# Two pads of a kernel's SBUF layout, 128 bytes shorter each

## The chip, the cores and the metric

The kernel runs on one core of a Trainium2 chip. The metric is device microseconds of one execution; lower is better. The time before is the median of three runs. The profile is of one further execution, whose own time stands beside it.

## The reference

The kernel computes a small decoder trunk on a residual stream x of 512 positions by 1024 features, in float32: one layer with a gated short convolution, one with forgetting attention, each followed by a feed-forward network (FFN) with a convolution.

```python
def short_conv_mixer(xn, w_in, conv_w, w_out):
    b, c, h = jnp.split(xn @ w_in, 3, axis=-1)
    return (b * causal_dwconv(c * h, conv_w)) @ w_out

def conv_ffn(xn, w_up, conv_w, w_down):
    a, g = jnp.split(xn @ w_up, 2, axis=-1)
    return (jax.nn.silu(causal_dwconv(a, conv_w)) * g) @ w_down
...
# layer 0: x += short_conv_mixer(rmsnorm(x)); x += conv_ffn(rmsnorm(x))
# before layer 1: k, v and the forget gate's cumulative decay c, all from h = rmsnorm(x)
# layer 1: x += (forgetting_attention(q, k, v, c) * sigmoid(gate)) @ w_out; x += conv_ffn(rmsnorm(x))
```

There are 16 heads of 64; the FFN is 2816 wide. Attention is a causal softmax of `q k / 8 + c_i - c_j`.

## The kernel before, in words

**Arithmetic.** TensorE multiplies float32 operands in a rounded form (F32R). To keep the precision, every operand is split into a rounded part `hi` and the rest `lo = x - hi`, and a product is three matmuls: hi x hi, hi x lo and lo x hi. ScalarE makes `hi` (a copy) and VectorE makes `lo` (a subtraction). For weights this is done in `parts` (L148 and L149), from a tile `raw` that a DMA filled.

**The matmuls.** Activations lie transposed, features on partitions and 512 positions along the row. `mac` (L164 to L166) adds one 128x128 block of weights times 128 features into a PSUM bank, in two halves of 256 columns, three matmuls each:

```python
nc.tensor.matmul(ps[:, f], lhsT=lh[0], rhs=rh[0][:, f], ...)   # L164
nc.tensor.matmul(ps[:, f], lhsT=lh[0], rhs=rh[1][:, f], ...)   # L165
nc.tensor.matmul(ps[:, f], lhsT=lh[1], rhs=rh[0][:, f], ...)   # L166
```

`lhsT` is the weights' tile that is loaded into the array, `rhs` the data that move through it. Every matmul loads its weights anew. The output projections of the mixer and of both FFNs use seven products in place of eight (`Seven`, the matmuls in `go`, L440 to L442, again three of 256 columns each, with weight splits at L423 and L424).

**Stages.** (1) The first three blocks of the mixer run as x arrives: weights are split into tiles of the pools g and gl, the moving data are the normed inputs n. (2) The rest of the mixer, its output projection, and the FFN of layer 0: weights in the pool w; the moving data are n for the input and up projections and g and gl for the output and down projections (each FFN has three down projections, after 7, 15 and 22 of the 22 column blocks of the up projection). (3) Attention: V is projected first, and there the roles are exchanged. The normed inputs n are the weights (slices of 128 columns) and the split weights, in pools whi and wlo, move, into four PSUM banks in turn. Then K, q and the gate are projected as in stage 2 with weights in whi and wlo and n or g as moving data, between the scores, the softmax and the products with V. (4) The FFN of layer 1, as in stage 2, with weights in w.

**Layout.** Pools take SBUF one behind the other, in the order in which they are opened. Those opened first stay: const, misc (m, ld), small, norm (tiles n, 2048 bytes per partition), raw (4096). Behind raw comes a set of pools for each stage, named with its number of tiles in `stage(...)`. A name that starts with pad is not a pool of tiles but so many bytes per partition that nothing uses. Tiles of g, gl, pt, s, whi and wlo have 2048 bytes per partition and those of w and sum 4096, all multiples of 256, as are the steps of a slice inside a tile (128 columns are 512 bytes). So where a tile starts modulo 256, counted from n, is set by the pads ahead of it alone.

**Order.** Outside of attention the order of the instructions of ScalarE, VectorE and GpSimd is held as written (`in_order`). `Line` loads weights and splits them some units ahead of their use (up to 12 tiles of w). TensorE takes the matmuls in the order in which they are written.

Of the kernel before, what the change touches and what calls it, by code (L numbers as in the profile page):

```python
# [57 lines left out]
def trunk(ctx: ExitStack, tc: tile.TileContext, x_t, a_in, a_out, up0, down0, wk, wv, wf, wqg, b_out,  # L58
# [14 lines left out]
    def stage(*sizes):  # L73

        pools = ExitStack()
        pool.clear()
        for name, bufs in sizes:
            if name.startswith("pad"):
                pools.enter_context(tc.tile_pool(name=name, bufs=1)).tile([P, bufs // 4], F32, tag=name,
                                                                          name=f"{name}_{len(pool)}_{len(sizes)}")  # L80
                continue
            pool[name] = pools.enter_context(tc.tile_pool(name=name, bufs=bufs))
        return pools
# [10 lines left out]
    def GL(dtype=F32):  # L94
        return new(pool["gl" if "gl" in pool else "g"], "gl" if "gl" in pool else "g", [P, T], dtype)
# [27 lines left out]
    pr = const.tile([P, NPAR], F32, tag="pr", name="pr")  # L123
    cs = const.tile([P, C_ET], F32, tag="cs", name="cs")

    pools = stage(("g", 16), ("sum", 4), ("gl", 16), ("pad", 192), ("w", 12))
    x = [GL() for _ in range(KT)]
    ones = const.tile([P, P], F32R, tag="ones", name="ones")
    nc.vector.memset(ones.bitcast(F32), 1.0)
# [158 lines left out]
    @contextmanager  # L288
    def in_order(*engines):

        traced = nc.cur_bb.bb.instructions
        n = len(traced)
        yield
        for eng in engines:
            own = [i for i in list(traced)[n:] if i.engine == eng.engine]
            for a, b in zip(own[:-1], own[1:]):
                tc.add_manual_dep(b, a.name, mybir.DependencyInfo(mybir.DependencyClass.NoSync,
                                                                  mybir.DependencyReason.DATA), reason="in order")
# [319 lines left out]
    def ffn_line(line, up, down):  # L618

        seq, k0 = [], 0  # L620
        for j in range(JT):
            seq.append(("up", j, [line.add(One(up[j, c])) for c in range(2)]))
            if j in (6, 14, JT - 1):
                n = (j + 1) // 2 - k0
                seq.append(("down", j, Project(line, [z[:, 4 * k0 * P:4 * (k0 + n) * P] for z in down], n)))
                k0 += n
        return seq

    def ffn(seq, col, norm, nxt, last=False):
        r = None  # L630
        us, late = [], None
        for kind, j, w in seq:
            if kind == "down":
                if j < JT - 1:
                    w.run(us, None)
                    us = []
                else:
                    late()
                    w.run(us, nxt, last=last, hold=True)
                continue  # L640
            if late:
                late()
                late = None
            if j == 0:
                pa, pg = gemm2(w, norm.xs, between=norm.fold)
                r, _ = norm.finish()
            else:
                pa = gemm(w[0], norm.xs)
            if j == JT - 1:
                part = seq[-1][2]  # L650
                part.prefetch()
            a = M()
            nc.vector.tensor_tensor(out=a, in0=pa, in1=r, op=ALU.mult)  # L653
            y = conv(a, col + 3 * j)
            act_silu(out=y, in_=y, func=AF.Silu)
            if j > 0:
                pg = gemm(w[1], norm.xs, j == JT - 1)
            g = M()
            nc.vector.tensor_tensor(out=g, in0=pg, in1=r, op=ALU.mult)  # L659
            if j % 2 == 0:  # L660
                f = S()

            def late(g=g, y=y, j=j, f=f):
                end = j == JT - 1
                (nc.vector if end else nc.gpsimd).tensor_tensor(out=half(f, j), in0=g, in1=y, op=ALU.mult)  # L665
                if j % 2:
                    us.append(operands(f, part.sevens[0].line.step if end else None))
# [481 lines left out]
        ffn(seq, PC_F[0], n2, n3)  # L1149
    pools.close()  # L1150
    n4 = Norm("ffn1")
    with stage(("pt", 6), ("s", 10), ("pad", 192), ("whi", 4), ("wlo", 4), ("pad2", 320), ("g", 40)):
        attention(n3, n4)
    with stage(("pad", 192), ("w", 12), ("pad2", 320), ("sum", 4), ("g", 16), ("gl", 16)):
        with in_order(*pinned):
            ffn(ffn_line(Line(12, 4), up1, down1), PC_F[1], n4, None, last=True)

# [76 lines left out]
```

## Time and profile before

| what | value |
|---|---|
| median of three runs | 1301.84 us (1297.83 to 1303.04) |
| profiled execution | 1303.14 us |
| its span, first to last instruction | 1301.4 us |
| mean granted TensorE clock | 0.978 of 2.4 GHz |
| TensorE busy | 1240.6 us, 95% of the span, 10113 matmuls |
| VectorE busy | 921.7 us, 71% |
| ScalarE busy | 593.7 us, 46% |
| GpSimd busy | 431.5 us, 33% |
| DMA | 151.40 MB, mean 116 GB/s |

The busy time of TensorE is a union of overlapping instructions: a matmul is recorded for some 280 ns, while the next one starts some 118 ns behind it. So busy time tells where TensorE has work; its pace is the distance of one start from the next. In a group's row `out<-in,in` names the tiles: the written one, then the moving one, then the weights.

### The profile page before, as it was taken

What the parts mean: (1) busy time and instruction counts of PE and PEld (TensorE: products, weight loads), DVE (VectorE), ACT (ScalarE), POOL (GpSimd) and SP (SyncE); (2) the same over time, 40 slices, a digit from 0 to 9 for tenths busy, and PEclk for the clock granted to TensorE, in tenths of its full rate; (3) what the DMA queues carried; (4) which work ended last, traced back from release to release, by engine and by line L of the source; (5) the groups of instructions that cost most, each with busy time, mean ns of one, the idle gap of its engine ahead of it and who ended that gap; (6) DMA issues with size and microseconds to landing.
All of it is one profiled execution on the core that took longest, in us unless ns stands there. A gap on an engine that the chain in (4) does not pass through costs nothing.

```text
span 1301.4 us, 24422 instructions
## 1 busy us (share of the span) xinstructions
PE 1240.6 (95%) x10113; PEld 1205.5 (93%) x10113; DVE 921.7 (71%) x1274; ACT 593.7 (46%) x972; POOL 431.5 (33%) x319
## 2 busy tenths in 40 slices
PE   8999989999999999869999989999999999999997
PEld 8999978999999999869998878889999999999987
DVE  6755696778667866785636778876567867776677
ACT  6322354344434443443456677774434433343422
POOL 0113371234135414470022354542023612361244
PEclk9999998999999999998999899999999999999989
DMA  7331154227323632253233222225421752164213
GB/s 273 106 108 66 50 181 159 70 62 268 115 72 97 223 119 66 81 162 117 86 106 119 80 68 65 66 82 174 151 86 38 229 168 82 49 216 160 63 50 121
DMA packets 54352, 151.40 MB, mean 116 GB/s; under 512 B 6049, under 2 KB 6561, under 8 KB 54241
## 3 DMA queue, kind: packets, MB, share of 16 engines
q1 hardware_dynamic: 53456, 148.47, 35.7%
q8 instruction: 79, 1.29, 0.4%
q10 hardware_dynamic: 720, 1.18, 0.2%
q14 instruction: 33, 0.26, 0.1%
q0 software_dynamic: 64, 0.20, 0.0%
HBM read 133.01 MB, written 16.81 MB: 115 GB/s over the span
## 4 chain that ended last, share of the span: by engine, by line
PE 71%; DVE 16%; ACT 6%; issue 3%; POOL 2%; DMA 1%; SPq 0%; DVEq 0%; ACTq 0%; POOLq 0%
PE st L166 11%; PE st L164 11%; PE st L165 11%; PE mm L164 8%; PE mm L166 8%; PE mm L165 8%; DVE w L424 6%; PE st L442 3%; PE st L440 2%; PE st L441 2%; DVE gl L555 2%; PE mm L442 1%; PE mm L440 1%; PE mm L441 1%; ACT s L305 1%
## 5 line engine op out<-in xcount | busy, mean ns | idle before, releaser
L164 PE MATMUL st<-n,w 128*128 128x256 f32 x1216 | 342.1, 281 | 3.7 <-ACT n L272 2.5
L166 PE MATMUL st<-n,w 128*128 128x256 f32 x1216 | 341.6, 281 | 0.8 <-DVE w L149 0.8
L165 PE MATMUL st<-n,w 128*128 128x256 f32 x1216 | 341.4, 281 | 0.2 <-DVE n L273 0.2
L164 PEld LDWEIGHTS st<-n,w 128*128 128x128 f32 x1216 | 229.9, 189 | 4.2 <-ACT n L272 2.7
L166 PEld LDWEIGHTS st<-n,w 128*128 128x128 f32 x1216 | 230.5, 190 | 1.0 <-DVE w L149 1.0
L165 PEld LDWEIGHTS st<-n,w 128*128 128x128 f32 x1216 | 229.8, 189 | 0.6 <-DVE n L273 0.5
L665 POOL TENSOR_TENSOR sum<-m,m 128x512 f32<-128x512 f32 x42 | 64.6, 1538 | 341.7 <-DVE m L659 273.2
L149 DVE TENSOR_TENSOR w<-raw,w 128x1024 fp32r<-128x1024 f32 x109 | 133.1, 1240 | 56.9 <-ACT w L148 56.8
L164 PE MATMUL mm<-n,w 128*128 128x256 f32 x528 | 147.6, 280 | 0.0
L166 PE MATMUL mm<-n,w 128*128 128x256 f32 x528 | 147.5, 279 | 0.0
L165 PE MATMUL mm<-n,w 128*128 128x256 f32 x528 | 147.3, 279 | 0.0
L440 PE MATMUL st<-g,w 128*128 128x256 f32 x460 | 131.0, 285 | 13.8 <-ACT m L453 11.9
L442 PE MATMUL st<-g,w 128*128 128x256 f32 x460 | 131.0, 285 | 3.6 <-DVE w L424 3.6
L148 ACT CAST w<-raw 128x1024 fp32r<-128x1024 f32 x109 | 111.1, 1042 | 50.8 <-DMA raw<-up 18.5
L470 ACT ACTIVATE m<-m,pr 128x512 f32<-128x512 f32 x52 | 37.7, 724 | 175.1 <-DVE m L653 137.2
L441 PE MATMUL st<-gl,w 128*128 128x256 f32 x393 | 111.1, 283 | 0.0
L440 PEld LDWEIGHTS st<-g,w 128*128 128x128 f32 x460 | 87.9, 191 | 15.4 <-ACT m L453 13.3
L166 PEld LDWEIGHTS mm<-n,w 128*128 128x128 f32 x528 | 99.2, 188 | 0.0
L165 PEld LDWEIGHTS mm<-n,w 128*128 128x128 f32 x528 | 99.0, 187 | 0.0
L164 PEld LDWEIGHTS mm<-n,w 128*128 128x128 f32 x528 | 99.0, 187 | 0.0
L376 ACT CAST g<-sum 128x512 fp32r<-128x512 f32 x78 | 48.4, 621 | 107.5 <-POOL sum L665 64.3
L424 DVE TENSOR_TENSOR w<-sum,w 128x1024 fp32r<-128x1024 f32 (+1 forms) x56 | 85.5, 1540 | 13.0 <-ACT w L423 13.0
(221 smaller groups left out, 3322.9 us busy)
## 6 DMA issues: line engine op xcount, KB each, us to landing
raw<-up SPq DMA_DIRECT2D x88, 512.0 KB, 4.3
ld<-xsp SPq DMA_DIRECT2D x64, 256.0 KB, 4.0
raw<-down SPq DMA_DIRECT2D x32, 512.0 KB, 3.6
xsp<-gl SPq DMA_DIRECT2D x48, 256.0 KB, 3.4
raw<-a_in SPq DMA_DIRECT2D x21, 512.0 KB, 4.4
raw<-wqg SPq DMA_DIRECT2D x16, 512.0 KB, 3.6
raw<-down SPq DMA_DIRECT2D x16, 384.0 KB, 3.2
raw<-a_out SPq DMA_DIRECT2D x8, 512.0 KB, 4.0
```

The costliest lines, as they stand in the source:

```text
L148: nc.scalar.copy(out=hi[:, :w], in_=raw[:, c0:c1])
L149: nc.vector.tensor_tensor(out=lo[:, :w], in0=raw[:, c0:c1], in1=hi[:, :w].bitcast(F32), op=ALU.subtract)
L164: nc.tensor.matmul(ps[:, f], lhsT=lh[0], rhs=rh[0][:, f], start=go, stop=False, skip_group_check=True)
L165: nc.tensor.matmul(ps[:, f], lhsT=lh[0], rhs=rh[1][:, f], start=False, stop=False, skip_group_check=True)
L166: nc.tensor.matmul(ps[:, f], lhsT=lh[1], rhs=rh[0][:, f], start=False, stop=end, skip_group_check=True)
L376: nc.scalar.copy(out=blocks(hi), in_=src)
L424: nc.vector.tensor_tensor(out=lo[:, 0:n], in0=raw[:, 0:n], in1=hi[:, 0:n].bitcast(F32), op=ALU.subtract)
L440: nc.tensor.matmul(ps, lhsT=wh, rhs=xh, start=m in "17" and p == 0, stop=False, skip_group_check=True)
L441: nc.tensor.matmul(ps, lhsT=wh, rhs=xl, start=False, stop=False, skip_group_check=True)
L442: nc.tensor.matmul(ps, lhsT=wl, rhs=xh, start=False, stop=p == self.n - 1, skip_group_check=True)
L470: nc.scalar.activation(out=y, in_=src, func=AF.Copy, scale=pr[:, col + 2:col + 3])
L665: (nc.vector if end else nc.gpsimd).tensor_tensor(out=half(f, j), in0=g, in1=y, op=ALU.mult)
```

## The change

All three sets of pools change, and in them only the pads: 64 bytes in place of 192, and 192 in place of 320 for the second pad. Tiles of w, whi and wlo lie 128 bytes lower by it, and in the last two stages those behind the second pad 256 bytes lower. The code of the computation is the same.

```diff
-    pools = stage(("g", 16), ("sum", 4), ("gl", 16), ("pad", 192), ("w", 12))
+    pools = stage(("g", 16), ("sum", 4), ("gl", 16), ("pad", 64), ("w", 12))
...
-    with stage(("pt", 6), ("s", 10), ("pad", 192), ("whi", 4), ("wlo", 4), ("pad2", 320), ("g", 40)):
+    with stage(("pt", 6), ("s", 10), ("pad", 64), ("whi", 4), ("wlo", 4), ("pad2", 192), ("g", 40)):
         attention(n3, n4)
-    with stage(("pad", 192), ("w", 12), ("pad2", 320), ("sum", 4), ("g", 16), ("gl", 16)):
+    with stage(("pad", 64), ("w", 12), ("pad2", 192), ("sum", 4), ("g", 16), ("gl", 16)):
```

## Rows read from the trace of the kernel before

**Rows 1.** The chain that ended last, shares of the span by engine, tile, line.

```profile
by line: PE st L166 10.8%; PE st L164 10.8%; PE st L165 10.7%; PE mm L164 8.0%; PE mm L166 7.9%; PE mm L165 7.9%; DVE w L424 5.9%; issue 3.4%; PE st L442 2.5%; PE st L440 2.5%; PE st L441 2.4%; DVE gl L555 1.8%; PE mm L442 1.4%; PE mm L440 
```

**Rows 2.** Span of the core and its mean granted TensorE clock.

```profile
core 0: 1301.4 us, clock 0.978
```

**Rows 3.** By stretch: length; PE, PEld, DVE, ACT, POOL busy (instructions); clock; DMA.

```profile
33.00:140.00 107.00, 107.00 (x909) 106.92 (x908) 63.23 (x80) 33.29 (x43) 22.44 (x12) 1.00 0.27 88
304.00:390.00 86.00, 85.31 (x724) 85.31 (x725) 61.88 (x76) 33.60 (x46) 19.91 (x14) 1.00 0.44 144
410.00:518.00 108.00, 107.19 (x897) 107.19 (x898) 77.03 (x89) 46.40 (x63) 38.98 (x25) 0.98 0.44 138
634.00:700.00 66.00, 66.00 (x530) 62.44 (x529) 35.35 (x53) 38.36 (x70) 12.61 (x9) 1.00 0.37 113
...
880.00:985.00 105.00, 103.07 (x855) 102.46 (x854) 66.73 (x82) 44.92 (x65) 21.64 (x15) 0.98 0.41 131
1026.00:1110.00 84.00, 83.62 (x710) 83.62 (x711) 60.18 (x76) 32.66 (x45) 19.89 (x14) 1.00 0.46 146
1132.00:1238.00 106.00, 105.51 (x884) 105.51 (x885) 74.43 (x89) 45.64 (x62) 38.44 (x24) 0.98 0.44 140
...
0.00:22.00 22.00, 17.91 (x107) 16.09 (x108) 14.91 (x28) 14.61 (x23) 0.93 (x5) 0.92 0.86 312
...
577.00:593.00 16.00, 6.91 (x38) 6.75 (x37) 12.23 (x17) 3.61 (x6) 5.33 (x5) 0.68 0.62 194
```

**Rows 4.** TensorE's waits: who waited for whom, us in total, times, longest.

```profile
PE st L164 <- ACT w L148: 1.2, 1, 1.2
...
PE st L166 <- DVE w L149: 0.8, 1, 0.8
```

**Rows 5.** Timeline of TensorE in the first mixer: start, duration; first and last.

```profile
22.66 0.28 PE L165 MATMUL st<-n,g 128*128 128x256 f32 x1
...
27.09 0.28 PE L166 MATMUL st<-n,gl 128*128 128x256 f32 x1
```

**Rows 6.** The same in the rest of the mixer, first and last.

```profile
59.74 0.28 PE L165 MATMUL st<-n,w 128*128 128x256 f32 x1
...
65.98 0.28 PE L164 MATMUL st<-n,w 128*128 128x256 f32 x1
```

**Rows 7.** The same in the projection of V, first and last.

```profile
611.81 0.28 PE L164 MATMUL st<-whi,n 128*128 128x256 f32 x1
...
617.93 0.28 PE L164 MATMUL st<-whi,n 128*128 128x256 f32 x1
```

**Rows 8.** Line L165 by tiles: duration ns min/median/max, first and last start.

```profile
L165 PE MATMUL st<-n,w x1216: 276/279/583, 27.7 to 1246.7; 128*128 128x256 f32 x174
...
L165 PE MATMUL mm<-n,whi x288: 276/279/415, 637.7 to 857.6; 128*128 128x256 f32 x144
...
L165 PE MATMUL st<-wlo,n x64: 276/276/415, 589.3 to 631.0; 128*128 128x256 f32 x64
...
L165 PE MATMUL st<-n,g x32: 280/283/415, 8.9 to 27.3; 128*128 128x256 f32 x32
```

**Rows 9.** Timeline of TensorE right behind the first mixer, first and last.

```profile
27.58 0.28 PE L164 MATMUL st<-n,w 128*128 128x256 f32 x1
...
32.45 0.28 PE L165 MATMUL st<-n,w 128*128 128x256 f32 x1
```

**Rows 10.** The chain from 0 to 27.6 us, shares of that stretch.

```profile
by line: DMA g<-a_in 21.3%; PE st L164 16.0%; PE st L166 14.5%; PE st L165 14.1%; PE mm L166 7.6%; PE mm L164 7.2%; PE mm L165 6.8%; ACT g L266 4.5%; SPq L1113 1.5%; SPq L1110 1.5%; SPq L1115 1.4%; issue 1.0%
```

**Rows 11.** The chain from 587 to 634 us (V), shares of that stretch.

```profile
by line: PE mm L165 17.5%; PE mm L166 16.6%; PE st L165 16.3%; PE mm L164 16.3%; PE st L166 16.2%; PE st L164 15.4%; DMA m<-cst 8.1%; PE st L736 0.7%; PE at L353 0.5%; PE at L352 0.5%
```

**Rows 12.** Splits on VectorE by line: duration ns min/median/max, first and last start.

```profile
L149 DVE TENSOR_TENSOR wlo<-raw,whi x64: 673/693/1789, 626.6 to 906.9; 128x512 fp32r<-128x512 f32 x64
...
L377 DVE TENSOR_TENSOR gl<-sum,g x78: 676/684/691, 53.7 to 1255.6; 128x512 fp32r<-128x512 f32 x78
```

**Rows 13.** The chain from 143 to 200 us, shares of that stretch.

```profile
by line: DVE w L424 23.3%; issue 13.6%; DVE gl L555 12.1%; DVE n L273 7.4%; DMA ld<-xsp 6.0%; DVE m L461 5.2%; DVE gl L564 4.9%; ACT n L272 3.7%; PE st L442 2.6%; POOL m L607 2.3%; DVE gl L377 2.1%; PE st L441 1.9%; ACT w L423 1.9%; PE st L
```

## The prediction

> **What bounds the kernel now.** I read the profile in four steps: what the chain that ended last consists of, at what pace TensorE runs where it is never kept waiting, on what that pace depends, and what else could become the bound.
>
> The chain [rows 1] is made of TensorE. The three matmuls of `mac` (L164 to L166) hold 10.8 + 10.8 + 10.7 + 8.0 + 7.9 + 7.9 = 56.1% of the span of 1301.4 us [rows 2]. Those of `Seven.go` (L440 to L442) hold the 2.5 + 2.5 + 2.4 + 1.4% shown and two groups cut off behind them, each at most 1.4%, which I take as 1.2% each: 11.2%. Together 67.3%, or 876 us. Nothing else in the row is over 5.9%.
>
> In the long stretches between the down projections TensorE does not wait. Seven of them, 662 us in all, hold 5509 matmuls, and TensorE is busy in 98% of each or more [rows 3]. For the weights' splits into w at L148 and L149, one wait of 1.2 and one of 0.8 us are recorded in the whole trace [rows 4]. So these stretches last as long as their matmuls are apart.
>
> The reader should now look at that distance, from one start to the next. All these matmuls have 256 columns and a fresh 128x128 weight tile, and run at the granted clock of 2.4 GHz. Yet there are three paces. The first mixer (moving n, weights in g and gl) takes 4.43 us for 37 steps, 119.7 ns [rows 5]. The rest of the mixer (moving n, weights in w) takes 6.24 us for 53 steps, 117.7 ns [rows 6]. The projection of V, where n is the weights and whi or wlo moves, takes 6.12 us for 54 steps, 113.3 ns [rows 7]. The recorded durations have the same order: medians 283, 279 and 276 ns, and 279 again for n against whi [rows 8].
>
> **On what the pace depends.** The three cases differ in where the tiles lie. From n to w there are pools whose tiles are multiples of 256 bytes, and one pad of 192. From n to whi it is the same, and both pads together (512) bring g back. So, counting how far the weights' tile lies behind the moving one, modulo 256: the first mixer has 0 and 119.7 ns; w, whi and wlo as weights have 192 and 117.7 ns; V, with the roles exchanged, has minus 192, which is 64, and 113.3 ns. The first two run the same function, three matmuls on the same moving n, and differ only in the weights' pool, so placement is the plainest reading of that difference.
>
> One stretch warns against reading too much into it. From 27.58 us on, right behind the first mixer, 43 steps with weights in w take 4.87 us: 113.3 ns at distance 192 [rows 9]. So that distance has two steady paces, the fast one rarely: the median of its 1216 `st` matmuls is 279, the minimum 276 [rows 8]. In V median and minimum are both 276. I read this as weights and moving data disturbing each other unless they run at a lucky offset in time, and V's distance as the one where that offset is the usual one.
>
> The Trainium skill speaks against any effect ("TensorE: Matmul & The Clock Gate", Part 2, step-by-step): TensorE has two independent read ports, and loading the next weights does not slow the matmul that runs. Its section on the back-to-back gap would put 256 columns at 109.2 ns wherever the tiles lie, and by it the time would not change. The trace disagrees: 113.3, 117.7 and 119.7 ns in the same six matmuls.
>
> **The change, part by part.** No instruction, transfer, wait or order changes; only addresses do.
>
> 1. Weights in w, whi and wlo go from 192 to 64 behind what moves (n in the mixer and the up projections, g and gl in the down projections, n and g in the attention; g stays a multiple of 256 behind n, since 64 + 192 = 256). That is V's distance of today. Scores, transposes and the products with V touch no tile of w, whi or wlo and keep their distances. I price each such matmul at 113.3 instead of 117.7 ns, 4.4 less. Not at that pace now are, of the chain's 876 us: the first mixer, 66.2% of 27.6 us, 18 us [rows 10]; V, 98.3% of 47 us, 46 us [rows 11]; and what runs at 1.2 GHz. The mean clock of 0.978 [rows 2] means about 0.044 x 1301.4 = 57 us at the low level; the start and the gap before V hold 3.5 + 10.2 of it [rows 3], 43 remain, much of it beside waits for VectorE; I count 30 on the chain (bounds 0 and 43), with no gain. That leaves 782 us at 117.7 ns, 6640 matmuls: 29.2 us.
>
> 2. V exchanges roles, so its distance goes from 64 to 192. About 41 of its 46 us run at 113.3 ns, 360 matmuls: 1.6 us lost (bounds 0 and 1.6).
>
> 3. VectorE and ScalarE write w at another place. The split of 128x512 takes 673 ns at best with its inputs 192 apart (raw and whi) and 676 with them 0 apart (sum and g) [rows 12], so I price this at nothing, both ways; if it cost the 3 ns, some 500 splits would add 1.5 us, nearly all off the chain.
>
> 4. What of the gain is lost to others. Around the down projections VectorE is the chain (23.3% L424, 12.1% L555 from 143 to 200 us [rows 13]); a faster TensorE waits longer there. The chain's share already leaves this out, but short TensorE pieces between such waits may gain nothing. The seven clean stretches alone give 5509 x 4.4 = 24.2 us. What lies outside them, 29.2 - 24.2 = 5 us, may be lost; I take 4 of it. In the clean stretches VectorE is busy 61.88 of 86 us (72%) in the fullest and would be at 75%, so nothing is late next there.
>
> Sum: 29.2 - 1.6 - 4 = 23.6 us. The profiled execution took 1303.14 us, so 1279.5; the median of the runs shown, 1301.84, lies 1.3 below it. Forecast: 1279 us, 1.8% faster.
>
> **The rivals.**
>
> A. The above, 1279 us. With nothing lost in 2 and 4, the profiled time less 29.2 and the median's 1.3 is 1272.6, and a run as low as the fastest shown (1297.83) would be near 1270. With half of the 27.6 lost it is 1288. For it: two differences of pace that follow placement. Against it: V differs in roles too, and it also changes its PSUM bank after six matmuls (the first mixer does so as well, at 119.7). Chance 0.74.
>
> B. Half gain: the fast pace is reached at distance 64 but falls back after waits, as it does at 192, or VectorE takes up half the gain after each down projection. 1288 to 1298, middle 1292. Against it: V's median is its minimum. Chance 0.08.
>
> C. No effect: V's pace comes from its roles. Its weights are slices of n, and one moving tile serves several weights in turn. Then w stays at 117.7 and V where it is: 1302 (1298 to 1303). For it: 113.3 ns also occurs at distance 192 [rows 9], so placement is not all. The Trainium skill's rule of separate ports, named above, gives the same. Chance 0.11.
>
> D. Slower: what counts is not the distance but where the weights start. Counted from n, weights have started at 0 (the first mixer and V) and at 192; a start at 64 occurs nowhere in this trace. If it is as bad as the worst pace seen, 119.7, each of the 6640 matmuls costs 2.0 ns more: 13.3 us, and V moves to 117.7: 1302 + 13 + 2 = 1317. It decides as soon as the new pace is over 118.7 ns (6640 x 1.0 = 6.6 us, 0.5%). Against it: V and the first mixer start their weights at the same place modulo 256 and are 6.4 ns apart, so the weights' start alone does not set the pace. Chance 0.07.
>
> **How the numbers follow.** 1279 is A's. A's own range is 1270 to 1288. A and B together hold 0.82, so the range runs from 1270 to B's end at 1298 and leaves out C, D and the edges of A. A measurement of this kernel tells about 0.5%, 6.5 us, from no change: faster is below 1295.3. A and most of B lie there: 0.81. C and the rest of B are within 0.5%: 0.12. D is slower: 0.07.
>
> **What would show it.** In the changed profile: the steps of the mixer and up matmuls 113.3 ns apart with a median duration of 276 instead of 279; `Seven.go` and the K and q projections the same; V 117.7 apart with 279 (that is the sharpest test of distance against roles); the first mixer unchanged at 119.7 and 283. VectorE's and ScalarE's durations stay within a few ns. TensorE's waits for VectorE around the down projections grow by a few us together. Wrong would be: w at 117.7 with V still at 113.3 (C), w at 119 or more (D), or w at 113.3 with TensorE's idle time grown by over 10 us (B).

## The result, and the profile after

The changed kernel takes 1285.37 us in the median of three runs (1282.35 to 1286.38), the kernel before 1301.84. The ratio is 0.9875 with a 95% interval of 0.9833 to 0.9918: 1.2% faster, of 1.8% forecast. The profiled execution took 1286.38 us.

The instructions and their order on each engine are the same as before. So the two traces can be laid side by side, matmul by matmul, and what differs is only when each one starts.

Span and clock, then the chain that ended last by line, of the kernel after (to [rows 1, 2]):

```profile
core 0: 1284.6 us, clock 0.984
```

```profile
by line: PE st L166 9.2%; PE st L164 9.1%; PE st L165 9.1%; PE mm L164 7.1%; PE mm L165 7.1%; PE mm L166 7.0%; DVE w L424 5.5%; issue 4.5%; PE st L442 2.6%; PE st L440 2.6%; PE st L441 2.6%; PE mm L442 1.4%; PE mm L440 1.4%; DVE gl L555 1.4
```

The span is 16.8 us shorter. The three matmuls of `mac` fall from 56.1 to 48.6% of the chain, which is what a faster TensorE would show. How fast, the durations of L165 by tile tell (to [rows 8]; ns min/median/max, then first and last start):

```profile
L165 PE MATMUL st<-n,w x1216: 276/276/419, 27.6 to 1230.1; 128*128 128x256 f32 x174
...
L165 PE MATMUL mm<-n,whi x288: 276/276/285, 628.4 to 844.2; 128*128 128x256 f32 x144
...
L165 PE MATMUL st<-wlo,n x64: 279/279/415, 579.7 to 621.5; 128*128 128x256 f32 x64
...
L165 PE MATMUL st<-n,g x32: 280/283/416, 7.5 to 27.2; 128*128 128x256 f32 x32
```

The medians have traded places: weights in w and whi went from 279 to 276, V (where wlo moves) from 276 to 279, and the first mixer stayed at 283. But a median hides how many stand on its other side. The timeline of TensorE at three places, first and last of each stretch (to [rows 6, 7]; the rest of the mixer, the up projection of layer 0 after 320 us, V):

```profile
59.81 0.28 PE L164 MATMUL st<-n,w 128*128 128x256 f32 x1
...
77.94 0.28 PE L165 MATMUL mm<-n,w 128*128 128x256 f32 x1
...
319.74 0.28 PE L165 MATMUL st<-n,w 128*128 128x256 f32 x1
...
337.99 0.28 PE L164 MATMUL mm<-n,w 128*128 128x256 f32 x1
...
596.79 0.28 PE L165 MATMUL mm<-wlo,n 128*128 128x256 f32 x1
...
616.93 0.28 PE L165 MATMUL st<-wlo,n 128*128 128x256 f32 x1
```

The first pair is 18.13 us for 160 steps, 113.3 ns: the pace that was forecast. The second is 18.25 us for 155 steps, 117.7 ns: the old pace, in the same code, at the same distance of 64, without a wait. The third is 20.14 us for 171 steps, 117.8 ns: V has the pace that the weights had.

So the weights run at two paces now. By long stretches (to [rows 3]: length, TensorE busy and matmuls, clock, DMA; a matmul that straddles an edge is counted too, so counts lie up to three above length over pace):

```profile
33.00:135.00 102.00, 102.00 (x900) 1.00 0.27 86
208.00:275.00 67.00, 67.00 (x594) 1.00 0.23 67
303.00:384.00 81.00, 81.00 (x690) 1.00 0.42 137
410.00:505.00 95.00, 95.00 (x841) 1.00 0.48 150
918.00:984.00 66.00, 66.00 (x584) 1.00 0.23 67
1013.00:1093.00 80.00, 80.00 (x681) 1.00 0.43 139
1125.00:1218.00 93.00, 93.00 (x792) 1.00 0.46 145
```

At 113.3 ns, 67 us hold 591 matmuls, and at 117.7 ns 569: the second stretch is fast. So are the first and the fourth. The third, sixth and seventh are slow (81 us would hold 715 and hold 690), and the fifth, after 918 us, is only partly fast. Two kinds of stretch and hardly anything between them; all of it at the full clock and with TensorE never idle.

For the rest of the text a matmul counts as fast if the next one starts at most 115 ns later, and slow if it starts 116 to 126 ns later. I counted this over every 256-column matmul with weights in w, whi or wlo that has its successor right behind it, some 8700 in each trace. Before, 113 of them were fast (1.3%) and their mean was 117.72 ns; after, 4959 (57%) and 115.26 ns.

Now add up the steps of TensorE, each from one start to the next. Steps of 256 columns that take at most 126 ns come to 20.0 us less than before (1084.1 to 1064.1). Steps that hold a wait come to 5.0 us more (69.8 to 74.7; the waits themselves grew from 56.6 to 60.8), and all others to 1.7 us less (141.4 to 139.7). Together that is the 16.8 us, but for rounding. Among the others, matmuls at the low clock (rows of ten or more steps of some 213 ns) are about as many as before, 160 against 156. The mean clock of 0.984 leaves out the start of the program: 24 of these 160 steps lie ahead of the first entry in the clock's record. Where the waits grew, the view of TensorE's waits shows, first the kernel before, then after (us in total, times, longest):

```profile
PE st L440 <- ACT m L453: 11.9, 7, 2.6
PE mm L165 <- DMA m<-cst: 9.1, 1, 9.1
PE mm L440 <- ACT m L453: 8.8, 5, 2.6
```

```profile
PE st L440 <- ACT m L453: 14.1, 7, 3.5
PE mm L440 <- ACT m L453: 10.5, 5, 3.1
PE mm L165 <- DMA m<-cst: 9.1, 1, 9.1
...
PE st L164 <- ACT w L148: 1.2, 1, 1.2
...
PE st L166 <- DVE w L149: 0.8, 1, 0.8
```

The twelve waits at the down projections, for the copy at L453 that empties a PSUM bank, are 3.9 us longer together; the waits for weights (to [rows 4]) are the same. The row of 9.1 us ahead of V is the same too, and it comes back below. The splits on VectorE did not move (to [rows 12]):

```profile
L149 DVE TENSOR_TENSOR wlo<-raw,whi x64: 673/693/1793, 617.0 to 892.8; 128x512 fp32r<-128x512 f32 x64
...
L377 DVE TENSOR_TENSOR gl<-sum,g x78: 678/685/691, 53.9 to 1238.9; 128x512 fp32r<-128x512 f32 x78
```

### The profile page after: what moved, and what is told of

It is laid out like the page before. It is cut to its first block, busy times and chain, and to the rows that moved or that the text cites. A ratio compares the mean times of both kernels' runs of the same rounds, so it can differ in the third digit from the quotient of the medians.

```text
span 1284.6 us, 24422 instructions
## 1 busy us (share of the span) xinstructions
PE 1219.7 (95%) x10113; PEld 1185.6 (92%) x10113; DVE 918.2 (71%) x1274; ACT 593.3 (46%) x972; POOL 432.8 (34%) x319
## 4 chain that ended last, share of the span: by engine, by line
PE 64%; DVE 20%; ACT 7%; issue 4%; POOL 2%; DMA 1%; SPq 0%; DVEq 0%; ACTq 0%; POOLq 0%
PE st L166 9%; PE st L164 9%; PE st L165 9%; PE mm L164 7%; PE mm L165 7%; PE mm L166 7%; DVE w L424 5%; PE st L442 3%; PE st L440 3%; PE st L441 3%; PE mm L442 1%; PE mm L440 1%; DVE gl L555 1%; PE mm L441 1%; DVE gl L377 1%
## 5 line engine op out<-in xcount | busy, mean ns | idle before, releaser
L165 PE MATMUL st<-n,w 128*128 128x256 f32 x1216 | 339.4, 279 | 0.4 <-DVE n L273 0.4
L165 PEld LDWEIGHTS st<-n,w 128*128 128x128 f32 x1216 | 230.7, 190 | 0.7 <-DVE n L273 0.6
L165 PE MATMUL mm<-n,w 128*128 128x256 f32 x528 | 146.8, 278 | 0.0
L165 PEld LDWEIGHTS mm<-n,w 128*128 128x128 f32 x528 | 99.7, 189 | 0.0
L424 DVE TENSOR_TENSOR w<-sum,w 128x1024 fp32r<-128x1024 f32 (+1 forms) x56 | 85.8, 1545 | 14.0 <-ACT w L423 13.9
```

The costliest lines, as they stand in the source:

```text
L165: nc.tensor.matmul(ps[:, f], lhsT=lh[0], rhs=rh[1][:, f], start=False, stop=False, skip_group_check=True)
L424: nc.vector.tensor_tensor(out=lo[:, 0:n], in0=raw[:, 0:n], in1=hi[:, 0:n].bitcast(F32), op=ALU.subtract)
```

## The experiments

**The same kernel again.** `again` is the changed kernel without an edit.

> The changed kernel unaltered, for a second profile and a closer ratio. State theory (at distance 64 TensorE has two steady paces, 113.3 and 117.7 ns; which one it is in is settled anew at each disturbance, a wait, a stretch at 1.2 GHz or a 512-column matmul, and then kept): the two paces again, with a fast share between 40 and 75%, but not all long stretches at the same pace as in the first profile; the time is 1278 to 1290 us and moves with that share by 4.4 ns per matmul. Rival, the pace belongs to the place in the program (which tiles, which stage): the same stretches fast and slow, the FFN of layer 0 fast before 302 us and from 410 to 520, that of layer 1 slow.

Measured: 1282.6 us (ratio 0.9878, 0.9856 to 0.99), span 1283.3 us. The gain repeats. The same windows of this second execution:

```profile
33.00:135.00 102.00, 102.00 (x900) 1.00 0.28 86
208.00:275.00 67.00, 67.00 (x572) 1.00 0.22 65
303.00:384.00 81.00, 81.00 (x717) 1.00 0.43 140
410.00:505.00 95.00, 95.00 (x809) 1.00 0.45 149
918.00:984.00 66.00, 66.00 (x582) 1.00 0.25 73
1013.00:1093.00 80.00, 80.00 (x681) 1.00 0.47 149
1125.00:1218.00 93.00, 93.00 (x823) 1.00 0.48 154
```

Compare the counts line by line. The first is the same; the second and fourth have turned slow (594 to 572, 841 to 809), the third and seventh fast (690 to 717, 792 to 823). It is the same program with the same tiles at the same addresses. So in these four the place in the program doesn't decide the pace; something that differs from one execution to the next does. How busy the DMA is does not tell the two paces apart: in the second stretch its share is 0.23 with the fast pace and 0.22 with the slow one. In total 5105 are fast here (59%).

**Other distances.** Four kernels change only the pads, so that the weights lie 128, 96, 32 or 0 bytes behind:

```diff
-("pad", 64) ... ("pad2", 192)
+("pad", 128) ... ("pad2", 128)     # pad128: V at 128 as well
+("pad", 96) ... ("pad2", 160)      # pad96: V at 160
+("pad", 32) ... ("pad2", 224)      # pad32: V at 224
+no pads                            # pad0: all at 0
```

> Pads of 128 and 128 bytes. 128 and -128 are the same modulo 256, so by the distance theory V and all the other projections must show the same pace or pair of paces here, as in no other layout but 0. If paces depend on roles or on the weights' start, V and the others still differ. Time by distance theory: 1276 if that pace is 113.3, 1302 if it is 117.7, 1315 if it is 119.7.

> Pads of 96 and 160 bytes: the weights' tiles lie 96 behind what moves, and in the projection of V the distance is -96, that is 160. Distance theory (each distance modulo 256 has its own steady paces): the mixer, up, down, K and q matmuls all show one new figure for 96, V another one for 160; nothing else changes. If 96 is a distance where only the fast pace is steady, nearly all are 113.3 ns apart and the time is near 1276; if only the slow one, 117.7 and 1302. Start theory (what counts is where the weights' tile starts, counted from the inputs n): V, whose weights start at n, keeps one pace whatever the pad is; it had 113.3 and 117.7 with the pads 192 and 64, so a third figure or one of the two says little, but a V that changes again speaks against it. Roles theory (V is fast by its roles): V at 113.3.

> Pads of 32 and 224 bytes: weights 32 behind what moves, V at 224. Distances seen so far: 0 119.9, 64 113.3 or 117.7, 96 118.2 in the mean, 128 118.7, 160 (V) 120.0, 192 117.7 with a rare 113.3. Distance theory alone can't name 32 and 224; if the pace changes smoothly between 0 and 64, 32 lies at 116 to 119 and the time near 1300. A pace under 113 at either distance would name a better layout.

> No pads: all of n, g, w, whi and wlo start at the same place modulo 256. Distance theory: everything, V too, runs at the first mixer's 119.7 ns with recorded durations of 283, so about 6640 matmuls x 2.0 ns more on the chain: 1302 + 13 + 2 (V) = 1317. If the first mixer was slow for another reason (it is at the start and fed by x as it arrives), the others stay at 117.7 or 113.3.

Measured: 1304.1 us for 128 (ratio 1.0037, 1.0016 to 1.0058), 1300.5 for 96 (1.0012, 0.9993 to 1.0031), 1302.3 for 32 (1.0033, 1.0017 to 1.0049) and 1302.58 for no pads (1.0017, 1.0 to 1.0034). None is a gain, and the 1317 us expected of no pads did not come either. The mean distance of starts, back to back, worked out from the starts in each trace:

| kernel | weights in w, whi, wlo: distance, ns | V: distance, ns | first mixer (0), ns |
|---|---|---|---|
| before | 192, 117.72 | 64, 113.48 | 119.90 |
| after | 64, 115.26 (57% fast) | 192, 117.79 | 119.89 |
| pad128 | 128, 118.72 | 128, 118.64 | 119.92 |
| pad96 | 96, 118.18 | 160, 119.97 | 119.88 |
| pad32 | 32, 118.31 | 224, 116.7 | 119.89 |
| pad0 | 0, 119.89 | 0, 119.95 | 119.89 |

With pads of 128 the distance is the same in both roles, and so is the pace. With no pads everything runs at the pace of the first mixer. That is the distance at work, and neither the function nor the roles. A distance of 64 is the best of the six tried for the weights, and the only one at which long stretches of them at 113.3 ns are common. At 32, 96 and 128 the steps go up and down between some 115 and 122 ns within each stretch, so there the means are no steady paces.

What the reader should not miss is that the kernel with no pads is hardly slower than before although its matmuls are: by 2.2 ns each, 19 us over 8700. It wins 9.5 us at the start of V. This is taken up below.

**Distance or start.** `shift128` is the kernel before with 128 bytes taken ahead of everything, so that all tiles start elsewhere modulo 256 and no distance changes:

```diff
+    const.tile([P, 32], F32, tag="shift", name="shift")
     pr = const.tile([P, NPAR], F32, tag="pr", name="pr")
```

> The pads of before (192 and 320), and 128 unused bytes ahead of all pools, so that every tile but the constants' first lies 128 bytes further: the weights then start where they start in the changed kernel (modulo 256), at the distances of before. Distance theory: the paces of before, 117.7 nearly everywhere and 113.3 in V, 1302 us. Start theory (an absolute place of the weights decides): the paces of the changed kernel, over half of the matmuls at 113.3, about 1285 us.

Measured: 1298.17 us (ratio 0.999, 0.9966 to 1.0014), V at 113.46 ns as before, the weights at 117.27. So 128 bytes more ahead of every tile changed neither pace, and the 1285 us of the start theory did not come. The last number is lower than 117.72 because one stretch, from 301 to 389 us, ran fast at distance 192: in 313 to 383 us there are 620 matmuls, where the kernel before has 596.

**Pushing TensorE out of step.** If the pace is settled at a disturbance, one can be made. Two matmuls of 512 columns into a bank that nobody reads stand ahead of the units 8 and 16 of both up projections, in the changed kernel (`kick64`) and in the one before (`kick192`):

```diff
+        if kick:
+            nothing = bank("at")
+            for _ in range(2):
+                nc.tensor.matmul(nothing, lhsT=unit.w[0][0], rhs=xs[0][0], start=True, stop=True)
...
-                pa = gemm(w[0], norm.xs)
+                pa = gemm(w[0], norm.xs, kick=j in (8, 16))
```

> The changed kernel with two idle matmuls of 512 columns (distance 64, into a bank that nobody reads) ahead of the units 8 and 16 of both up projections. In the first profile of the changed kernel 12 of 13 slow stretches that met 512-column matmuls where nothing else disturbed them came out fast, and 6 of 10 fast ones stayed fast. State theory: behind each of the four pairs the long stretch (some 850 to 1000 matmuls) is fast in most cases, the fast share rises from 57% to 75 to 90%, that is 1700 to 2900 matmuls x 4.4 ns = 7 to 13 us gained against 4 x 0.47 = 1.9 us paid: 1274 to 1280 us. Rival (the pace belongs to the place, or such matmuls don't set it): fast share as before, 1285 to 1288.

> The same four pairs of idle matmuls in the kernel before, with the pads of 192 and 320. Distance sets which state a disturbance leads to: at 192, 26 of 27 slow stretches stayed slow behind 512-column matmuls, so the pace stays 117.7 and the time is 1302 to 1304. If the idle matmuls themselves made the fast pace, whatever the distance, the up projections would run at 113.3 here too and the time would fall by 10 us or more.

Measured: `kick64` 1282.87 us (ratio 0.9872, 0.985 to 0.9894), no better than the changed kernel alone; `kick192` 1294.94 us (0.9981, 0.9955 to 1.0006). In `kick64` two of the four kicks met a fast stretch and left it fast, one turned slow into fast, one left slow slow; 65% of the matmuls are fast, short of the 75 to 90% expected. The steps of at most 126 ns take 4.4 us less than in the changed kernel; the four idle pairs and a few more steps at the low clock (172 against 160) took that back. `kick192` was to stay slow and did not: in both layers the kick at unit 8 turned slow into fast for some 700 matmuls each. The kick at unit 16 left slow slow in both. The timeline of `kick192` around the first one:

```profile
321.76 0.28 PE L166 MATMUL st<-n,w 128*128 128x256 f32 x1
321.88 0.28 PE L164 MATMUL st<-n,w 128*128 128x256 f32 x1
322.00 0.28 PE L165 MATMUL st<-n,w 128*128 128x256 f32 x1
322.11 0.28 PE L166 MATMUL st<-n,w 128*128 128x256 f32 x1
322.23 0.62 PE L246 MATMUL at<-n,w 128*128 128x512 f32 x2
322.69 0.28 PE L164 MATMUL st<-n,w 128*128 128x256 f32 x1
322.81 0.28 PE L165 MATMUL st<-n,w 128*128 128x256 f32 x1
322.92 0.28 PE L166 MATMUL st<-n,w 128*128 128x256 f32 x1
323.03 0.28 PE L164 MATMUL st<-n,w 128*128 128x256 f32 x1
323.14 0.28 PE L165 MATMUL st<-n,w 128*128 128x256 f32 x1
323.26 0.28 PE L166 MATMUL st<-n,w 128*128 128x256 f32 x1
```

Ahead of the kick four starts are 0.12, 0.12 and 0.11 us apart (117.7 ns); from 322.92 on three steps take 0.34 us (113.3). The windows either side of it, of the same kernel:

```profile
313.00:322.00 9.00, 9.00 (x79) 1.00 0.87 315
323.00:400.00 77.00, 77.00 (x682) 1.00 0.29 89
```

682 matmuls in 77 us is the fast pace (680; the slow one would give 654). So both paces exist at both distances, and 64 makes the fast one likelier. Of the six kicks that met the slow pace, all three at unit 8 turned it fast and none of the three at unit 16 did; no kick turned fast into slow, but the pace falls back elsewhere (in `kick192` at 1018.4 us, where TensorE waits between two matmuls that start 1.6 us apart). Neither kernel gained by its kicks beyond the noise, so they are no lever here.

`kick192` shows the same of V, whose distance is 64 there. It starts slow and turns fast behind the transposes at L740, at 602.5 us:

```profile
589.00:602.00 13.00, 13.00 (x111) 1.00 0.32 100
604.00:629.00 25.00, 25.00 (x223) 1.00 0.32 105
```

In all, 239 of its 366 steps are fast.

**The stall ahead of V.** The kernel with no pads takes 9.5 us less than the kernel before across the start of V. The sizes of the pools say why. In stages 1 and 2, g takes 32768 and sum 16384 bytes, so the first gl tile starts at 49152. In stage 3, pt, s, whi and wlo take 12288 + 20480 + 8192 + 8192 = 49152, plus the pad: with any pad, the last wlo tile ends 32 to 192 bytes inside a gl tile of the stage before. The idea is that V's first splits can't be placed ahead of the release of that tile. `gap64` is the changed kernel, `gap192` the one before, each with 256 bytes more between sum and gl:

```diff
-    pools = stage(("g", 16), ("sum", 4), ("gl", 16), ("pad", 64), ("w", 12))
+    pools = stage(("g", 16), ("sum", 4), ("pad0", 256), ("gl", 16), ("pad", 64), ("w", 12))
```

> The changed kernel with 256 bytes more between the pools sum and gl of stages 1 and 2, so that the first gl tile starts at 49408 bytes behind the pools' base in place of 49152, and the last wlo tile of stage 3 (which ends at 49152 plus the pad, 49216) no longer reaches into it. All distances modulo 256 stay. Theory (the first weight splits of V wait for the free of that gl tile, since 64 bytes of the last wlo tile lie in it): the splits at L717 start some 5 us earlier, the gap of some 9 us ahead of V is gone and the low clock behind it too, as in the kernel with no pads, where this stretch took 9.5 us less; the time falls from the changed kernel's 1283 to about 1274 (1270 to 1278). The projection of V stays at 117.8 ns, the weights in w, whi and wlo at a mixture of 113.3 and 117.7 ns. Rival (the gap comes from something else that the missing pads changed, such as the pace of the matmuls ahead of it): the gap stays at 9 us and the time at 1283 (1279 to 1286).

> The kernel before with the same 256 bytes more between sum and gl: the last wlo tile ends at 49344, short of the first gl tile at 49408. Theory of the overlap: 9 us less than before, 1290 (1287 to 1294), with w, whi and wlo at 117.7 and V at 113.3 ns as before. Rival (the gap has another cause): no change, 1300. If both kernels gain the same 9 us, gap and pace are separate matters and the 128 bytes less in the pads bought only pace.

Measured: `gap64` 1269.89 us (ratio 0.9783, 0.9756 to 0.981), `gap192` 1289.5 us (0.9916, 0.9884 to 0.9948). Between the 4400th matmul of the program, ahead of stage 3, and the 4700th, in V, `gap64` gains 9.6 us on the kernel before and `gap192` 10.0; the changed kernel gains 0.7 there. The 1269.89 us lie just below the 1270 to 1278 expected, and V did not stay at 117.8 ns in `gap64`: 142 of its 381 steps are fast, all ahead of 587.6 us, and the mean is 116.12 at a distance of 192. VectorE's timeline, the changed kernel first and then `gap64` (start, us, line, tiles):

```profile
574.08 1.60 DVE L273 SCALAR_TENSOR_TENSOR n<-gl,pr,n 128x512 fp32r<-128x512 f32 x1 [0.38 <-ACT n L272]
575.77 1.58 DVE L717 TENSOR_TENSOR wlo<-raw,whi 128x512 fp32r<-128x512 f32 x1
```

```profile
563.94 1.22 DVE L555 TENSOR_TENSOR gl<-ld,m 128x512 f32<-128x512 f32 x1
565.08 0.68 DVE L717 TENSOR_TENSOR wlo<-raw,whi 128x512 fp32r<-128x512 f32 x1
565.68 0.41 DVE L556 TENSOR_TENSOR gl<-gl,st 128x256 f32<-128x256 f32 x1
```

In the changed kernel VectorE splits V's first weights at 575.77 us, behind the norm of the last blocks; in `gap64` the first split stands at 565.08, between two steps of the residual. So the order of VectorE's instructions has changed. Compared by line and tiles with the kernel before, VectorE's order is the same in the changed kernel, pad32, pad96 and pad128, which all have the overlap, and differs at 21 places in pad0, `gap64` and `gap192`, which have none: V's first four splits stand earlier. That goes with the overlap in all eight kernels; how the overlap sets the order is not shown, since of the four wlo tiles only the last reaches into the gl tile, and all four splits move. TensorE, 25 us around the start of V, the changed kernel and then `gap64`:

```profile
565.00:590.00 25.00, 15.91 (x123) 0.86 0.56 171
```

```profile
565.00:590.00 25.00, 22.68 (x190) 1.00 0.66 214
```

The row of 9.1 us is gone from the waits of both kernels. It had named a transfer as the releaser, `m<-cst`, and in `again`, the same program, another one:

```profile
PE mm L165 <- DMA m<-wf: 9.2, 1, 9.2
```

A releaser that changes from execution to execution, for a matmul that reads neither tile, is a coincidence in time. L165 moves wlo, and wlo's split was what came last.

**Does the share of fast matmuls set the time?** Two more profiles of `gap64`:

> The kernel gap64 unaltered, for a second profile. Its first profiled execution (span 1277.7 us) had 4434 of some 8700 back-to-back matmuls with weights in w, whi and wlo at 113.3 ns and was the longest of its executions; the others took 1268 to 1272. Theory (the time of one execution is set by how many matmuls keep the fast pace, and this is settled anew at each disturbance): a span shorter by x us comes with about x / 3.5 ns more fast matmuls, so near 1268 us some 7000 of them; and stretches that were fast in the first profile may be slow in this one. Rival (executions differ by waits and by the granted clock): the same stretches fast, 4400 of them, at any span.

> The same kernel once more, a third profile, with the same two expectations: by the theory the fast count follows the span at 3.5 ns for each matmul, by the rival it stays at 4400 whatever the span.

Measured: 1271.69 and 1273.65 us, spans 1269.9 and 1271.9. The long stretches of all five executions at a distance of 64, as fast matmuls in a hundred (worked out from the starts; the times at the heads are those of the kernel after, the stretches of the others are the same matmuls):

| execution | mixer 42-139 | up 209-270 | up 299-389 | up 417-506 | up 901-965 | up 997-1087 | up 1111-1209 | fast in all | span, us |
|---|---|---|---|---|---|---|---|---|---|
| after | 100 | 100 | 4 | 100 | 82 | 0 | 0 | 4959 | 1284.6 |
| again | 100 | 0 | 99 | 0 | 82 | 0 | 97 | 5105 | 1283.3 |
| gap64 | 100 | 0 | 99 | 0 | 82 | 18 | 0 | 4434 | 1277.7 |
| gap64_2 | 100 | 100 | 99 | 0 | 82 | 18 | 97 | 5821 | 1269.9 |
| gap64_3 | 100 | 0 | 99 | 100 | 20 | 100 | 2 | 5550 | 1271.9 |

The rest of the mixer is fast in all five, and the stretch from 901 us on is 82% fast in four, so chance does not set everything; what stands behind the first down projections differs each time. Within `gap64` the span follows the count: 1387 more matmuls at the fast pace for 7.8 us, 1116 for 5.8, about 5.4 ns each, where 3.5 had been expected; waits differ by under 2 us (53.8, 52.1, 53.6). A fast step is only 4.4 ns shorter than a slow one, so part of the difference has other sources. The rival, equal counts at different spans, is out, though the slope was off, and three executions are few to fit one.

## Why the prediction was right, and where it was off

**Step 1, the pace by distance: right in kind, off in size.** The weights took on V's pace, 113.3 ns to the tenth, but 57% of them, not all: 54% in the mixer and the up projections, 56% in `Seven.go`, 69% in K, q and the gate. The step that failed is "I read this as ... V's distance as the one where that offset is the usual one": V's 346 fast of 355 was one stretch of 46 us, and I priced 6640 matmuls from it. Of the 38.3 us that 8700 matmuls at 4.4 ns would be worth, 21.4 came (8696 x (117.72 - 115.26)). A second error went the other way: I counted only the 6640 on the chain that I could place at 117.7 ns, but all 8696 took part, and all but 3.2 us of the 20.0 came through to the span. The two errors offset each other in part: 1279 and 1285 are closer than the reasons for them, and that is luck. The front's own rows had the warning [rows 9]: a distance with two paces. I applied it to 192 alone.

**Step 2, V: right.** 117.79 ns instead of 113.48; 368 steps make 1.6 us, as priced. Together with pad128 it refutes rival C: the roles have no part in it. That V has one steady pace at either distance did not hold in later runs (`gap64`, `kick192`).

**Step 3, the splits: right.** 673/693 and 678/685 ns, nothing beyond 2 ns.

**Step 4, losses to others: right in size.** TensorE waits 4.2 us more, 4 were taken; the waits at L453 alone grew by 3.9 us. What they wait for there is a copy by ScalarE. The prediction had named VectorE, but the waits for its splits at L424 did not grow (6.4 and 6.1 us).

**Rival B** named part of what happened, the fast pace that falls back. But its place was wrong: it falls back at some disturbances and comes up at others, and its price (1288 to 1298) assumed at most half. **Rival D** is out by pad0 and shift128. Its own price would also have been too high: pad0 shows 19 us of slower matmuls, but TensorE's waits fell from 56.6 to 43.8 us in all, most of it at the earlier start of V, and its rows of steps at the low clock from 156 steps to 87, each some 93 ns longer than a step at 119.9.

The Trainium skill ("TensorE: Matmul & The Clock Gate", Part 2, step-by-step) says that loading the next weights takes no read bandwidth from the matmul that runs. The prediction set this against the three paces, and the runs bear the paces out: the same matmul with the same load goes at 113.3, 117.7 or 119.9 ns in kernels whose pads differ by a few hundred bytes at most. That a matmul at a distance of 64 or 192 bytes goes at either pace is not explained by it either. The 109.2 ns that the prediction took from the section "Back-to-back issue gap" of the same page of the Trainium skill is, as that section says, the gap of a matmul by itself, without the load of weights that each matmul here has. No long stretch here came down to it.

**Open.** What in the chip makes the two paces, and what at a disturbance decides for one. That the weights' reads and the moving data's reads fall into step with each other would fit a dependence on distance and on chance, but no run here shows those reads. Nor is it explained why V at a distance of 64 kept the fast pace nearly throughout in before, shift128 and gap192, and for 239 of 366 steps in kick192, while of the weights at that distance 51 to 67% were fast, or why the kicks at unit 8 worked and those at unit 16 did not. Distances that are no multiple of 32 were not tried.

## What to carry to other kernels

Where TensorE runs back to back and loads weights for every matmul, measure the distance of starts in each stretch, not busy time or medians, and try the distance between the moving and the stationary tile modulo 256 as a parameter; here the pace ran from 113 to 120 ns with it, at 256 columns. Before a pace seen in one stretch is priced into thousands of matmuls, look whether another execution of the same program has it in the same place. And when pads shift pools, look which tile of the next stage reaches over into one still in use: 64 bytes cost the changed kernel 8.9 us here, more than half of what the pads bought, and `gap64` takes 1269.89 us, 2.2% less than the kernel before.

## What the runs showed of the hardware that was not expected

- TensorE has two steady paces for the same 256-column matmuls with a weight load each, 113.3 and 117.7 ns, at a distance of 64 and of 192, and can keep one for 1000 matmuls (1003 at 113.3 ns from 34.0 us on in the kernel after). Two matmuls of 512 columns switched it from slow to fast in three cases of six.
- At a distance of 0 there is hardly any such choice: 26 of some 8700 were fast, at a mean of 119.89 ns.
- With no pads, TensorE's matmuls were slower and fewer of them ran at the low clock: 87 steps of some 213 ns in rows of ten or more, where the kernel before has 156, at a mean granted clock of 0.987 against 0.978. With shorter waits this paid for 19 us of slower matmuls, and the span is the same within 0.1 us. How much of it comes from the pace and how much from the changed order ahead of V is not separated.
